# First pairs of a down projection loaded into the places of their low parts, the last column gated behind the visits, no activation sums on GpSimd

## The chip, the cores and the metric

One core of a Trainium2 chip runs the whole program. The metric is device time of one execution in microseconds; three runs of the kernel before gave 2354.93 to 2358.16, median 2356.17. Besides these there is one execution under the profiler.

## The reference, cut to what matters

One layer of a hybrid encoder over 512 + 16 prompt positions and 8 x 16 sample positions, all in float32. The change is in the last sub-layer, a convolutional gated MLP of width 5632 = 44 columns of 128:

```
up = rmsnorm(x, g_ffn) @ w_up                    # 2048 -> 2 x 5632
g, v = up[..., :D_FF], up[..., D_FF:]
gc = conv_b + sum_k gext[:, k:k + seqlen] * conv_w[k]    # causal depthwise conv, width 3
h = gelu(gc) * v
x = x + h @ w_down                               # 5632 -> 2048
```

then a final rmsnorm. Activations lie as 128 features by 640 positions (two halves of 320; the up stage carries two more columns, 322).

## The kernel before, in words

**Exact products.** Each float32 operand is split into a high part, rounded to the matmul's reduced format, and a low part, the difference; hi x hi, hi x lo and lo x hi make three matmuls. ScalarE writes the high part (`S.copy`), VectorE subtracts for the low part. For weights these are the tiles `wh` and `wl` (four buffers each) from the raw tiles `wraw` (four) and `wr` (six), each raw tile being 128 x 512 and 256 KB.

**Seven products instead of eight.** The up projection treats the input as eight pairs of feature blocks and multiplies by a Winograd scheme: seven chains (`CHAINS`) of eight pairs for the gate and value parts of a column. The seven activation combinations are kinds B11, T1, B21, B22, T3, T2, T4, kept split: pairs 0 to 5 in `XT` (pair, high or low, kind), 6 and 7 in `XH`. The weight sums P1 = A21 + A22, P3 = A11 + A21, P2 = P1 + A11, P4 = P2 + A12 are formed on VectorE in `Up.add`, four units ahead of use, and split three units ahead (a unit is half a chain, four pairs). A column is 7 x 2 x 4 x 3 = 168 matmuls. Only when P4 is formed is A11's buffer given to the next column's A11 (`free`, `load`).

**Gate.** When a column's value and gate parts are out of PSUM (`evict_up`), `gate` multiplies by the norm's scale, runs the convolution and GELU on VectorE and ScalarE, and `early` stores the column h[f] to DRAM (`h_d`) through GpSimd's queue. `gating` counts these; there are NFF = 44.

**Down projection, four parts in this order.**
- Head: columns 32 to 35 directly, 16 output rows x 4 columns x 6 matmuls = 384. `evict_head` copies a finished row from PSUM on ScalarE, `send` adds it into DRAM (`x3_d`, in the trace x_d) with an accumulating DMA on GpSimd's queue; `rows` counts.
- Sixteen visits: columns 0 to 31 as 16 pairs in the same scheme. A visit computes a pair of output rows from eight pairs; visit s uses pairs s to s + 7, so each visit brings one new pair into the place of the oldest. It has 168 matmuls of 320. The first visit runs its units in another order: first halves of five chains, then the second halves.
- REST: columns 36 to 39 directly, 384 matmuls of 320, rows evicted into `acc`.
- Tail: columns 40 to 43 in two halves of 384 and 256 positions, then the final norm.

**Where the first pairs come from.** `load_pair` takes two of the eight buffers `f26` and loads h[2p] and h[2p + 1]; `pair` forms T1, then T2, T3, T4 and splits all seven kinds into the pair's places, each behind `past(...)`, the point where column 43's matmuls have read what stood there. For pairs 0 to 9 the first sum and the split of B21 and B22 are on GpSimd (`e = G if p < KP + 2`). `some_pairs` runs two chains of three pairs; `later_pairs` does pairs 6 and 7, with GpSimd's first sums, when the head has sent eight rows and the last column is gated.

**What sets the order.** The program is written out by generators. `E.now` is the writer's estimate of the time; `E.until(E.now + 6)` holds the use of a load back by 6 us, `V.idle()` and `V.done()` hold work back while VectorE's estimated queue is long. Each engine executes its own instructions strictly in that order, as does SP, which issues nearly all loads. `room(n, gates)` waits until the next n buffers of the ring `f26` are free, and two more if gates are still to come.

Of the kernel before, what the change touches and what calls it, by code (L numbers as in the profile page):

```python
# [283 lines left out]
def body(tc, A):  # L284
# [40 lines left out]
    with tc.manual_schedule():  # L325
# [977 lines left out]
        class Up:  # L1303
# [32 lines left out]
            def add(self, u):  # L1336
                if u >= self.end:
                    return
                f, c, h = UN[u]
                p = CHAINS[c][0]  # L1340
                r = lambda n: R[f, n, h]
                if p == "P1":
                    if f == 0:
                        R[f, "P1", h] = r("A21")
                    elif f <= NFF:
                        self.put(f, "P1", h, "wraw")
                    if f <= NFF:
# [122 lines left out]

        def room(n=1, gates=False):

            while any(fl[0] + i - fpool[1] in live for i in range(n + 2 * (gates and gating[0] < NFF))):
                yield

        def let(hold):
            live.difference_update(hold)
# [39 lines left out]
        def early(f, g, v, hold):  # L1517
            while gating[0] < f:
                yield
            yield from room(2)  # L1520
            yield from gate(f, g, v, hold)
            nc.gpsimd.dma_start(out=h_d[f], in_=v[:, 0:640])  # L1522
            let(hold)
            gating[0] += 1

# [128 lines left out]
        def pair(p):  # L1654
# [22 lines left out]
            built[0] += 1  # L1677

        def some_pairs(ps):
            yield from past(-1, 2, 0)  # L1680
            yield from load_pair(ps[0])
            for p, nxt in zip(ps, ps[1:] + [None]):
                E.spawn(pair(p), 0, True)
                yield from past(-1, 6, KP - 1)
                if nxt is not None:
                    yield from load_pair(nxt)

        built = [0]
        head_at = [0]
        copied = [0]  # L1690
        rowt = [None]

        def later_pairs():
            while len(xy) < 6:
                yield
            for p in (6, 7):
                yield from load_pair(p)
# [3 lines left out]
            def two(ty, src, eng=V):  # L1701
                return split_kind([(kd(p, 0, ty), kd(p, 1, ty)) for p in (6, 7)], src, {(p, ty): p for p in (6, 7)}, eng)

            (x6, y6, hold6, _), (x7, y7, hold7, due) = xy[6], xy[7]
            xs, ys = (x6, x7), (y6, y7)
            yield from E.until(due)
            while rows[0] < 8 or gating[0] < NFF:
                yield
            place(0, B11)
            gx = fpool[0].tile([128, 18, 40], F32, tag="gx", name="gx", bufs=1).rearrange("p t b -> p (t b)")  # L1710
            t4 = gx[:, 0:320], gx[:, 320:640]
            for x in xs:
                TT(x[:, 1], x[:, 0], x[:, 1], SUB, G)
            yield from two(B11, [x[:, 0] for x in xs])
            while head_at[0] < 1:
                yield
            place(1, T1)
            yield from two(T1, [x[:, 1] for x in xs])
            for x, y, t in zip(xs, ys, t4):
                STT(x[:, 1], x[:, 1], -1.0, y[:, 1], MUL, SUB)  # L1720
                TT(t, x[:, 1], y[:, 0], ADD)
                TT(x[:, 0], x[:, 1], x[:, 0], ADD)
            while head_at[0] < 4 or rows[0] < 12:
                yield
            for i, ty, src in ((2, T4, t4), (3, T3, [x[:, 0] for x in xs]), (4, T2, [x[:, 1] for x in xs]),
                               (5, B21, [y[:, 0] for y in ys]), (6, B22, [y[:, 1] for y in ys])):
                place(i, ty)
                yield from two(ty, src)
            let(hold6 + hold7)
# [6 lines left out]

        def evict_head(n, ps):
            hold = []
            if n < 12:
                while rows[0] < n - 5:  # L1740
                    yield
                if n % 2 == 0:
                    rowt[0] = xhp.tile([128, 2, 2 * XW], F32, tag=f"xh{(0, 5, 6)[n // 2 % 3]}", name="rowt", bufs=1)
# [10 lines left out]
        def head():  # L1754

            for n in range(16):
# [20 lines left out]
        for u, (f, c, h) in enumerate(UN):  # L1777
# [54 lines left out]
            if f == NFF - 1 and h and 1 <= c <= 4:  # L1832
                load_h(HEAD[c - 1], xhp.tile([128, 2, 2 * XW], F32R, tag=f"xh{c}", name="hida", bufs=1))
                E.spawn(first_h(HEAD[c - 1], E.now + 5.5))
                if c == 1:
                    for i in range(2):
                        E.spawn(some_pairs([i, i + 2, i + 4]))
                    E.spawn(later_pairs())
# [16 lines left out]
        D = {}  # L1855

        def feed():
            while gating[0] < NFF or rows[0] < 16 + 2 * NV2:
# [18 lines left out]
            for f in last:  # L1877
                yield from split_h(f)

        E.spawn(feed())  # L1880

# [215 lines left out]
```

## Time and profile before

| | us |
|---|---|
| median of three runs | 2356.17 |
| the profiled execution | 2358.56 |
| its span, first to last instruction | 2356.8 |
| matmul engine (PE) busy | 2293.6 (97%) |
| VectorE (DVE) busy | 1869.7 (79%) |
| ScalarE (ACT) busy | 1060.2 (45%) |
| GpSimd (POOL) busy | 442.9 (19%) |
| pair loads `f<-h_d`, issue to landing, median of 46 | 4.6 |

Mean granted clock is 0.99 of full speed. PE's busy time is modelled from the starts of pipelined matmuls, so waits are read from its idle time and its clock. All matmuls and nearly all elementwise instructions share one helper line each (L164, L137); they are told apart by tiles: `pu` is a PSUM bank of the up stage, head and visits, `md` and `me` of REST and tail, `hida` and `hidb` hold split hidden columns, `f` is a buffer of the ring `f26`. Times in rows are us from the span's start. Column 42 starts at 1691.72, column 43 at 1716.38, the head at 1743.12, visit 0 at 1809.00, visit 1 at 1845.02, visit 2 at 1872.41, REST at 2225.20, the tail at 2281.75.

### The profile page before, as it was taken

Reading aid. Unit: us, or ns where it says so; the run is one execution under the profiler, and the core shown is the slowest. Engines: PE = TensorE matmul, PEld = TensorE weight load, DVE = VectorE, ACT = ScalarE, POOL = GpSimd, SP = SyncE. Lnnn points to the kernel's source line nnn. Section 1 sums busy time; section 2 is a strip of 40 time slices with the busy share of each in tenths; the row PEclk is TensorE's granted clock in tenths of the full one; section 3 lists DMA queues with packets and bytes.
Section 4 is the critical chain, followed back from the end, with each engine's and each line's share of the span. In section 5 each row is a group of like instructions: output and inputs, shape, how many; then the busy total and the mean of one; then the engine's idle time right before and its main releaser. Section 6 shows DMA issues by size and latency. Waiting matters only on the chain.

```text
span 2356.8 us, 41521 instructions
## 1 busy us (share of the span) xinstructions
PE 2293.6 (97%) x15440; PEld 2276.6 (97%) x15440; DVE 1869.7 (79%) x3084; ACT 1060.2 (45%) x1879; POOL 442.9 (19%) x640
## 2 busy tenths in 40 slices
PE   9998989999999999999999999999998899999997
PEld 9998989999999999999999999999998899999997
DVE  7589988646698888888888888888886777777646
ACT  6233443334454444444444444444454444444435
POOL 4755534200000000000000000000023211111013
PEclk9999999999999999999999999999999999999999
DMA  5323344444433333333333333333367777777643
GB/s 190 119 79 86 108 138 145 150 127 158 163 107 99 105 94 108 92 102 108 90 101 102 97 107 90 102 107 93 99 183 167 180 180 169 183 180 173 178 156 111
DMA packets 168699, 302.00 MB, mean 128 GB/s; under 512 B 22960, under 2 KB 43568, under 8 KB 168496
## 3 DMA queue, kind: packets, MB, share of 16 engines
q1 hardware_dynamic: 150784, 260.55, 35.6%
q0 software_dynamic: 17568, 38.79, 9.1%
q8 instruction: 121, 1.98, 0.3%
q14 instruction: 82, 0.67, 0.1%
q10 hardware_dynamic: 144, 0.01, 0.0%
HBM read 245.42 MB, written 53.85 MB: 127 GB/s over the span
## 4 chain that ended last, share of the span: by engine, by line
PE 78%; DVE 4%; issue 2%; ACT 1%; DMA 1%; POOL 0%; SPq 0%; DVEq 0%; POOLq 0%; ACTq 0%
PE pu L164 62%; PE mm L164 9%; PE mf L164 2%; PE me L164 2%; PE md L164 2%; DVE wl L137 1%; DVE f L137 1%; PE yps L164 1%; ACT wh L137 0%; POOL ssq L137 0%; ACT f L137 0%; DMA wr<-wup 0%; DVE acc L137 0%; PE vps L164 0%; DVE XT L137 0%
## 5 line engine op out<-in xcount | busy, mean ns | idle before, releaser
L164 PE MATMUL pu<-XT,wh 128*128 128x320 f32 (+1 forms) x5040 | 1125.1, 310 | 11.5 <-DVE f L137 8.2
L164 PEld LDWEIGHTS pu<-XT,wh 128*128 128x128 f32 x5040 | 847.4, 189 | 15.7 <-issue 10.2
L164 PE MATMUL pu<-XT,wl 128*128 128x320 f32 (+1 forms) x2520 | 781.9, 310 | 2.5 <-DVE wl L137 2.4
L137 ACT CAST wh<-wr 128x512 fp32r<-128x512 f32 x594 | 368.8, 621 | 543.6 <-PE pu L164 331.3
L137 DVE TENSOR_TENSOR wl<-wr,wh 128x512 fp32r<-128x512 f32 x594 | 411.8, 693 | 141.2 <-ACT wh L137 135.1
L164 PEld LDWEIGHTS pu<-XT,wl 128*128 128x128 f32 x2520 | 476.1, 189 | 4.4 <-DVE wl L137 4.4
L137 ACT CAST wh<-wraw 128x512 fp32r<-128x512 f32 (+1 forms) x423 | 260.2, 617 | 442.6 <-PE pu L164 159.9
L137 DVE TENSOR_TENSOR wl<-wraw,wh 128x512 fp32r<-128x512 f32 (+1 forms) x423 | 308.1, 730 | 172.2 <-ACT wh L137 168.2
L164 PE MATMUL mm<-H,wh 128*128 128x320 f32 (+2 forms) x1920 | 375.3, 317 | 12.2 <-ACT H L137 8.3
L164 PEld LDWEIGHTS mm<-H,wh 128*128 128x128 f32 x1920 | 307.3, 192 | 15.9 <-ACT H L137 8.5
L164 PE MATMUL pu<-XH,wh 128*128 128x320 f32 (+1 forms) x1232 | 276.9, 310 | 0.0
L164 PE MATMUL mm<-H,wl 128*128 128x320 f32 x960 | 223.8, 315 | 0.0
L164 PEld LDWEIGHTS pu<-XH,wh 128*128 128x128 f32 x1232 | 207.0, 189 | 0.0
L164 PE MATMUL pu<-XH,wl 128*128 128x320 f32 (+1 forms) x616 | 190.2, 309 | 0.0
L137 DVE TENSOR_TENSOR wr<-wr 128x512 f32<-128x512 f32 x236 | 162.3, 688 | 3.4
L164 PEld LDWEIGHTS mm<-H,wl 128*128 128x128 f32 x960 | 164.8, 191 | 0.0
L1499 POOL DMA_DIRECT2D cvo<-gx x44 | 31.9, 725 | 523.1 <-DVE gx L137 523.1
L137 DVE SCALAR_TENSOR_TENSOR f<-f,f 128x640 f32<-128x640 f32 (+2 forms) x161 | 123.3, 766 | 2.6 <-ACT f L137 0.8
L164 PEld LDWEIGHTS pu<-XH,wl 128*128 128x128 f32 x616 | 116.4, 189 | 0.0
L1522 POOL DMA_DIRECT2D h_d<-f x44 | 25.1, 571 | 454.4 <-DVE f L137 442.3
L137 DVE TENSOR_TENSOR wr<-wraw,wr 128x512 f32<-128x512 f32 x120 | 82.1, 684 | 0.1
L137 DVE SCALAR_TENSOR_TENSOR f<-gx,vec,f 128x640 f32<-128x640 f32 x88 | 78.8, 895 | 1.4
(299 smaller groups left out, 2890.8 us busy)
## 6 DMA issues: line engine op xcount, KB each, us to landing
wr<-wup SPq DMA_DIRECT2D x356, 256.0 KB, 2.9
wraw<-wts SPq DMA_DIRECT2D x195, 256.0 KB, 2.8
wraw<-wup SPq DMA_DIRECT2D x152, 256.0 KB, 2.8
f<-h_d SPq DMA_DIRECT2D x46, 320.0 KB, 4.6
h_d<-f POOLq DMA_DIRECT2D x44, 320.0 KB, 2.5
x_d<-f POOLq DMA_DIRECT2D x36, 320.0 KB, 4.5
wraw<-wup POOLq DMA_DIRECT2D x30, 256.0 KB, 4.3
w<-yg_d SPq DMA_DIRECT2D x16, 328.0 KB, 3.3
```

Of the source, the lines that this page charges most:

```text
L137: return f(*a, **k)
L164: return self.eng.matmul(out=out, lhsT=lhsT, rhs=rhs, start=start, stop=stop, **more)
L1499: nc.gpsimd.dma_start(out=A["cvo"][:, f], in_=gx[:, 16:18, 31:40])
L1522: nc.gpsimd.dma_start(out=h_d[f], in_=v[:, 0:640])
```

## The change

- `first_loads` / `first_load`: pairs 0 to 5 are loaded by SP straight into the pair's own places in `XT`: h[2p] into the low parts of B11 and T1 once column 43's second chain is through, h[2p + 1] into the low parts of T2 and T4 after its fifth chain has passed the pair; one pair every six units. Pairs 6 and 7 go, in eight loads of 160 KB, into `XH` places that the head's columns don't use, after column 43.
- `some_pairs` then forms the sums on VectorE into two ring buffers and splits the kinds; B11, B21 and B22 are split from where they were loaded. `later_pairs` waits for eleven sent rows, and spreads T1, T4, T3, T2 over the last head row.
- No sum or split of activations stays on GpSimd (`pair` and `later_pairs` use VectorE).
- `evict_head` takes its rows from the ring `f26` throughout, where it used three pairs of rows in `XH` places.
- P1 of the first visit is no longer summed on VectorE but by two loads on SP and two accumulating DMAs on GpSimd's queue (`Up.sum`), written at head row 13.
- Column 43: `early` stores its gate and value parts to DRAM (`u_d`); `last_gate`, started by `feed` at the start of REST, loads them, gates them and stores h[43], which is then loaded and split for the tail. The late ring has seven buffers instead of eight.

```diff
@@ Up.add
-                    elif f <= NFF:
+                    elif f < NFF:
                         self.put(f, "P1", h, "wraw")
-                    if f <= NFF:
+                    if f < NFF:
                         TT(r("P1"), r("A21"), r("A22"), ADD)
@@ room
-            while any(fl[0] + i - fpool[1] in live for i in range(n + 2 * (gates and gating[0] < NFF))):
+            while any(fl[0] + i - fpool[1] in live for i in range(n + 2 * (gates and gating[0] < NFF - 1))):
@@ early
+            if f == NFF - 1:
+                yield from V.done()
+                nc.gpsimd.dma_start(out=u_d[0][:, 0:640], in_=v[:, 0:640])
+                nc.gpsimd.dma_start(out=u_d[1][:, 0:2 * XW], in_=g.rearrange("p a c -> p (a c)"))
+                let(hold)
+                return
+        def last_gate():
+            hold = []
+            v, g = f26(hold), f26(hold)
+            SP.dma_start(out=v[:, 0:640], in_=u_d[0][:, 0:640])
+            SP.dma_start(out=g, in_=u_d[1][:, 0:2 * XW])
+            yield from E.until(E.now + 7)
+            yield from gate(NFF - 1, half2(g), v, hold)
+            nc.gpsimd.dma_start(out=h_d[NFF - 1], in_=v[:, 0:640])
+            let(hold)
+            gating[0] += 1
@@ pair
-            e = G if p < KP + 2 else V
-            TT(x[:, 1], x[:, 0], x[:, 1], SUB, e)
-            yield from e.done()
+            TT(x[:, 1], x[:, 0], x[:, 1], SUB)
+            yield from V.done()
...
-            yield from some(p, B21, y, e)
+            yield from some(p, B21, y)
@@ new, and some_pairs
+        def first_load(p):
+            f32 = lambda a, b: XT[:, p, 1, a:b, 0:320].bitcast(F32)
+            yield from past(-1, 1, p)
+            SP.dma_start(out=f32(B11, T1 + 1), in_=half2(h_d[2 * p]))
+            yield from past(-1, 4, p)
+            SP.dma_start(out=f32(T2, T4 + 1), in_=half2(h_d[2 * p + 1]))
+            xy[p] = f32(B11, T1 + 1), f32(T2, T4 + 1), None, E.now + 6
+        def first_loads():
+            for p in range(6):
+                yield from first_load(p)
+                yield 6
+            yield from past(-1, 6, 7)
...
         def some_pairs(ps):
+            for p in ps:
...
+                x, y, _, due = xy[p]
+                yield from E.until(due)
+                hold = []
+                yield from room(2, True)
+                a, b = (half2(f26(hold)[:, 0:640]) for _ in range(2))
+                TT(a[:, 0], x[:, 0], x[:, 1], SUB)
+                STT(b[:, 1], a[:, 0], -1.0, y[:, 1], MUL, SUB)
+                yield from V.idle()
+                TT(b[:, 0], b[:, 1], x[:, 0], ADD)
+                TT(a[:, 1], b[:, 1], y[:, 0], ADD)
...
@@ later_pairs
-            while rows[0] < 8 or gating[0] < NFF:
+            while rows[0] < 11 or 7 not in xy:
                 yield
...
-            while head_at[0] < 4 or rows[0] < 12:
-                yield
+            for i, ty, t in ((1, T1, t1), (2, T4, t4), (3, T3, t3), (4, T2, t2)):
+                while head_at[0] < i:
+                    yield
                 place(i, ty)
+                yield from two(ty, [t[:, 0], t[:, 1]])
@@ evict_head
-            if n < 12:
-                while rows[0] < n - 5:
-                    yield
...
-                t = rowt[0][:, n % 2]
-            else:
-                yield from room()
-                t = f26(hold)
+            yield from room(1, True)
+            t = f26(hold)
@@ head, at row 13
                     for half in range(2):
                         up.load(NFF, "A22", half)
+                    for half in range(2):
+                        up.sum(NFF, "P1", half, "A21", "A22")
@@ feed
-            fpool[1] = 8
+            fpool[1] = 7
...
-            last = range(REST[0] + 6, NFF)
-            for f in last:
-                load_h(f)
+            load_h(NFF - 2)
+            E.spawn(last_gate())
             yield from E.until(E.now + 7)
...
+            while gating[0] < NFF:
+                yield
+            load_h(NFF - 1)
+            yield from E.until(E.now + 7)
+            yield from split_h(NFF - 1)
```

## Rows read from the trace of the kernel before

**Rows 1.** Windows by stage: length; PE, PEld, DVE, ACT, POOL busy (x); PEclk, DMA, GB/s.

```profile
1691.72:1716.38 24.66, 24.66 (x170) 24.66 (x169) 21.70 (x35) 11.51 (x20) 2.07 (x4) 1.00 0.34 101
1716.38:1743.12 26.74, 24.99 (x170) 24.75 (x169) 24.17 (x38) 14.21 (x24) 3.88 (x6) 1.00 0.60 210
1743.12:1809.00 65.88, 60.26 (x386) 59.27 (x385) 43.98 (x59) 34.73 (x73) 27.37 (x28) 0.95 0.76 186
1809.00:1845.02 36.02, 28.22 (x170) 26.22 (x169) 27.95 (x50) 16.41 (x35) 7.81 (x9) 0.91 0.66 161
1845.02:1872.41 27.39, 25.23 (x171) 24.76 (x169) 23.33 (x37) 13.26 (x23) 6.41 (x6) 1.00 0.66 157
1872.41:2225.20 352.79, 349.28 (x2354) 346.26 (x2353) 271.76 (x466) 166.21 (x289) 46.97 (x54) 1.00 0.72 174
2225.20:2281.75 56.55, 56.55 (x386) 56.55 (x385) 25.48 (x36) 12.98 (x21) 0.86 (x1) 1.00 0.61 190
```

**Rows 2.** Timeline of PE: start, length, instruction, [idle before <- releaser].

```profile
1739.49 0.54 PE L164 MATMUL pu<-XT,wh 128*128 128x320 f32 x2 [1.75 <-DVE f L137]
...
1796.16 0.90 PE L164 MATMUL pu<-hida,wl 128*128 128x320 f32 x2 [4.76 <-DVE wl L137]
...
1839.95 0.87 PE L164 MATMUL pu<-XT,wh 128*128 128x320 f32 x2 [5.93 <-DVE f L137]
...
1856.91 0.41 PE L164 MATMUL pu<-XT,wh 128*128 128x320 f32 x1 [1.44 <-DVE XT L137]
```

**Rows 3.** Windows of 10 us around the head's long wait, same columns.

```profile
1790.00:1800.00 10.00, 5.24 (x24) 4.99 (x23) 8.11 (x6) 2.75 (x5) 5.54 (x5) 0.77 0.70 166
1800.00:1810.00 10.00, 9.45 (x57) 9.19 (x56) 1.81 (x1) 2.58 (x7) 3.38 (x5) 0.89 0.50 125
```

**Rows 4.** Timelines of DVE and POOL before that wait ended.

```profile
1789.24 1.62 DVE L137 TENSOR_TENSOR f<-f,f 128x320 f32<-128x320 f32 x1
1790.79 5.31 DVE L137 TENSOR_TENSOR wl<-wraw,wh 128x512 fp32r<-128x512 f32 x1
...
1791.07 4.47 POOL L137 TENSOR_TENSOR XT<-f,XT 128x640 fp32r<-128x640 f32 x3
```

**Rows 5.** Groups by form in the head: count | busy us, mean ns | idle before.

```profile
L137 DVE TENSOR_TENSOR XT<-f,XT 128x640 fp32r<-128x640 f32 x11 | 9.7, 886 | 5.5 <-ACT XT L137 5.5
...
L137 DVE TENSOR_TENSOR f<-f 128x320 f32<-128x320 f32 x5 | 2.5, 492 | 0.2
```

**Rows 6.** Timelines of DVE, SP's queue and ACT in visit 0.

```profile
1830.81 0.69 DVE L137 TENSOR_TENSOR wr<-wr 128x512 f32<-128x512 f32 x1
...
1831.87 0.33 SPq L1310 DMA_DIRECT2D wr<-wup  x1
...
1837.54 0.62 ACT L137 CAST wh<-wr 128x512 fp32r<-128x512 f32 x1 [3.30 <-DMA wr<-wup]
```

**Rows 7.** Timeline of ACT in column 43.

```profile
1736.24 0.73 ACT L137 CAST hida<-hida 128x640 fp32r<-128x640 f32 x1 [2.63 <-DMA hida<-h_d]
...
1737.39 0.42 ACT L137 COPY u<-pu 128x320 f32<-128x320 f32 x1
```

**Rows 8.** DMA issues from 1715 to 1870: count, KB each, median us to landing.

```profile
f<-h_d SPq DMA_DIRECT2D x22, 320.0 KB, 6.1
...
wraw<-wup POOLq DMA_DIRECT2D x4, 256.0 KB, 4.3
```

**Rows 9.** Timelines of DVE (the last column's gate), ACT and PE (REST and tail).

```profile
1747.76 0.89 DVE L137 TENSOR_TENSOR gx<-f,rstd 128x640 f32<-128x640 f32 x2
...
1759.48 1.68 DVE L137 SCALAR_TENSOR_TENSOR f<-f,f 128x640 f32<-128x640 f32 x2 [0.82 <-ACT f L137]
...
2240.01 0.73 ACT L137 CAST hida<-hida 128x640 fp32r<-128x640 f32 x1 [7.17 <-DMA hida<-h_d]
...
2288.05 0.69 PE L164 MATMUL me<-hidb 128*128 128x384 f32 x3
```

**Rows 10.** Waits of POOL from 1720 to 1870: us in total, times, longest.

```profile
POOL f L137 <- DMA f<-h_d: 34.0, 6, 10.4
```

More of the change, by code (lines that the diff above doesn't have):

```diff
@@ L1674, in pair @@
             yield from V.idle()
-            yield from some(p, B21, y, e)
+            yield from some(p, B21, y)
             let(hold)
-            built[0] += 1
-        def some_pairs(ps):
[L1680 to L1686, printed above, removed]
@@ L1688, in body @@
-        built = [0]
+        def first_load(p):
[10 more added lines that the diff above has]
+            yield from past(-1, 6, 7)
+            raw = lambda ty, i, h: XH[ty][:, i, h, 0:320].bitcast(F32)
+            for i in range(2):
+                x, y = h_d[2 * (6 + i)], h_d[2 * (6 + i) + 1]
+                x0, x1, y0, y1 = raw(B11, i, 1), raw(B11, i, 0), raw(B21, i, 1), raw(B22, i, 1)
+                for o, t, c in ((x0, x, 0), (x1, x, 320), (y0, y, 0), (y1, y, 320)):
+                    SP.dma_start(out=o, in_=t[:, c:c + 320])
+                xy[6 + i] = x0, x1, y0, y1, E.now + 6
@@ new lines, in some_pairs @@
+        def some_pairs(ps):
+            for p in ps:
+                while p not in xy:
+                    yield
[9 more added lines that the diff above has]
+                TT(a[:, 1], b[:, 1], y[:, 0], ADD)
+                yield from V.idle()
+                yield from some(p, B11, x[:, 0:1])
+                yield from V.idle()
+                yield from some(p, T1, a[:, 0:1])
+                yield from past(-1, 6, p)
+                yield from V.idle()
+                yield from some(p, B21, y)
+                yield from V.idle()
+                yield from some(p, T3, b)
+                yield from V.idle()
+                yield from some(p, T4, a[:, 1:2])
+                let(hold)
@@ L1689, in body @@
         head_at = [0]
         copied = [0]
-        rowt = [None]
         def later_pairs():
-            while len(xy) < 6:
-                yield
-            for p in (6, 7):
-                yield from load_pair(p)
             def place(i, ty):
                 XH[ty] = xhp.tile([128, 2, 2, XW], F32R, tag=f"xh{i}", name=f"XH{ty}b", bufs=1)
[L1701 to L1706, printed above, removed]
-            while rows[0] < 8 or gating[0] < NFF:
-                yield
[L1709 to L1715, printed above, removed]
-                yield
[L1717 to L1722, printed above, removed]
-            while head_at[0] < 4 or rows[0] < 12:
-                yield
-            for i, ty, src in ((2, T4, t4), (3, T3, [x[:, 0] for x in xs]), (4, T2, [x[:, 1] for x in xs]),
-                               (5, B21, [y[:, 0] for y in ys]), (6, B22, [y[:, 1] for y in ys])):
@@ new lines, in two @@
+            def two(ty, src):
+                return split_kind([(kd(p, 0, ty), kd(p, 1, ty)) for p in (6, 7)], src, {(p, ty): p for p in (6, 7)})
+            while rows[0] < 11 or 7 not in xy:
+                yield
+            yield from room(4)
+            hold = []
+            t1, t2, t3, t4 = (half2(f26(hold)[:, 0:640]) for _ in range(4))
+            for i in range(2):
+                x0, x1, y0, y1, due = xy[6 + i]
+                yield from E.until(due)
+                TT(t1[:, i], x0, x1, SUB)
+                STT(t2[:, i], t1[:, i], -1.0, y1, MUL, SUB)
+                yield from V.idle()
+                TT(t3[:, i], t2[:, i], x0, ADD)
+                TT(t4[:, i], t2[:, i], y0, ADD)
+                yield from V.idle()
@@ L1727, in later_pairs @@
+            lo = lambda ty: [XH[ty][:, i, 1, 0:320].bitcast(F32) for i in range(2)]
+            yield from V.done()
+            yield from two(B11, lo(B11))
+            for i, ty, t in ((1, T1, t1), (2, T4, t4), (3, T3, t3), (4, T2, t2)):
+                while head_at[0] < i:
+                    yield
                 place(i, ty)
-                yield from two(ty, src)
-            let(hold6 + hold7)
+                yield from two(ty, [t[:, 0], t[:, 1]])
+            let(hold)
+            for ty in (B21, B22):
+                yield from two(ty, lo(ty))
@@ L1738, in evict_head @@
             hold = []
-            if n < 12:
-                while rows[0] < n - 5:
-                    yield
-                if n % 2 == 0:
-                    rowt[0] = xhp.tile([128, 2, 2 * XW], F32, tag=f"xh{(0, 5, 6)[n // 2 % 3]}", name="rowt", bufs=1)
-                t = rowt[0][:, n % 2]
-            else:
-                yield from room()
-                t = f26(hold)
+            yield from room(1, True)
+            t = f26(hold)
             for (o, w), p in zip(HP, ps):
@@ L1835, in body @@
                 if c == 1:
+                    E.spawn(first_loads())
                     for i in range(2):
@@ L1857, in feed @@
         def feed():
-            while gating[0] < NFF or rows[0] < 16 + 2 * NV2:
+            while gating[0] < NFF - 1 or rows[0] < 16 + 2 * NV2:
                 yield
@@ L1872, in feed @@
             E.spawn(rest_acc())
-            last = range(REST[0] + 6, NFF)
-            for f in last:
-                load_h(f)
+            load_h(NFF - 2)
+            E.spawn(last_gate())
             yield from E.until(E.now + 7)
-            for f in last:
-                yield from split_h(f)
+            yield from split_h(NFF - 2)
+            while gating[0] < NFF:
+                yield
+            load_h(NFF - 1)
+            yield from E.until(E.now + 7)
+            yield from split_h(NFF - 1)
         E.spawn(feed())
```

## The prediction, made before the changed kernel ran

> **What bounds the kernel now.** I read the page first: the matmul engine is busy 97% of the span, so a change can only win where it stands still or runs at the lower clock. The windows cut at the program's stages come next [rows 1]. Column 42 is an undisturbed column of the up stage: 24.66 us. The last column, 43, takes 26.74. The direct part ("head") of the down stage takes 65.88, but the later direct part of columns 36 to 39 does the same 384 matmuls of 320 columns without a wait in 56.55. The first visit takes 36.02, the second 27.39; visits 2 to 15 take 352.79 / 14 = 25.20 each. The excess is 2.08 + 9.33 + 10.82 + 2.19 = 24.42 us, all in the 156 us that the change edits. That is the most it can win there; the visits behind keep their shape.
>
> Then the matmul engine's own waits [rows 2]: 1.75 us in column 43, 4.76 in the head, 5.93 in visit 0, 1.44 in visit 1, each put down to VectorE. After a wait the clock falls: the 10 us around the long head wait were granted 0.77 of full speed and the next ten 0.89 [rows 3], 81 matmuls where two full slices hold about 140. The missing 59, at 24.66/170 = 0.145 us, are 8.6 us: nearly all of the head's excess is this one wait and its slow echo.
>
> **The head: sums leave GpSimd.** The late instruction is one weight subtraction on VectorE that lasts 5.31 us, beside three GpSimd subtractions of 4.47 us together that began 0.28 us later; the sum just before it took 1.62 us against 0.49 on average for its shape [rows 4, 5]. The change puts every such subtraction on VectorE, so this stretch, the 4.76 wait and the slow clock behind it go. What comes instead: six two-part subtractions at 0.82 to 0.89 us (5.3) and, with the eight first sums, 8 x 0.49 (3.9) [rows 5].
>
> Is there room on VectorE? It is busy 43.98 us in the head [rows 1]. From that go the 8.5 us or so by which instructions ran longer beside GpSimd (4.6 and 1.1 in [rows 4], 1.2 for each of two in the gate and for a weight split, 0.3 at the end), and the last column's gate, 5.9 us (seven instructions of 0.8 to 0.9). To the rest, 29.6, come 4.9 + 2.5 of GpSimd's work inside the stage, six sums of pairs 6 and 7 (2.9), four of their seven splits (3.6), and 2 to 3 us of pairs 0 and 1 done in column 43 so far: 46 us of 56.55. It fits with 10 us over. I leave 2.5 us of the 9.33: 1.0 for first sums in front of a load not yet landed, 1.0 for the first visit's P1 (below), 0.5 at the ends. Bounds: 0.5 (all hidden) and 9.3 (as now).
>
> **P1 of visit 0** was two VectorE sums (0.7 each, one stretched to 1.3); it becomes two loads on SP and two accumulating DMAs on GpSimd's queue, issued at row 13 of 16. They need the weight buffers that the last two head chunks hold, so SP stands until VectorE has split these, and GpSimd's queue, with the row stores behind it, stands until each load has landed. An accumulating load of this size lands 4.3 us after issue here [rows 8]. With chunk 14 split about 12 us before the head's end, a load of some 4 and an accumulation of 4.3 to 5, P1 arrives 2 to 3 us before its split must begin: bounds 0 and 4 us of wait, I take 1.0. The Trainium skill ("DMA: Bandwidth & Descriptors", Anatomy of one DMA) puts a GpSimd DMA at 2.0 us plus its bytes over 436 GB/s, which for 256 KB is an estimated 2.6 us. The rows show 4.3, and by the page's figure the 1.0 would be 0.
>
> **Visit 0.** The chain of its long wait [rows 6]: VectorE forms the last weight sum (A12 + P2) at 1830.81; only that frees the buffer into which SP loads the next visit's A11 at 1831.87; the cast of it on ScalarE waits 3.30 us for the landing and starts at 1837.54, and the copy of a finished bank stands behind this cast, VectorE's combination behind that, and the matmuls behind that. In program order the weight sum belongs beside the unit that starts 14 us into the visit (about 1824.5 with the early waits); it came some 6 us late, behind VectorE's own queue (27.95 us busy in this visit [rows 1], nearly all before the wait). From there go P1's sums (2.0), six sums of pairs 6 and 7 (2.9), three or four of their splits at 0.89 (3.1), and stretched instructions (2.5): 10 us. Then the load is issued in time, and what is left is the short order of this visit: the copy and three VectorE operations, 1.8 us, against one unit of 1.76 us between. I leave 3.0 of 10.82. Bounds: 0.3, and 10.8 if the load is late for another reason.
>
> **Column 43.** The finished bank's copy came at 1737.39, behind a cast that waited 2.63 us for a hidden column's load [rows 7]. That load queued behind four pair loads (320 KB each); in the changed order one pair half stands ahead of it, the second halves come after chain 4, and then one pair every six units. A few hundred KB less is about 1 us. I leave 1.0 of 2.08; bounds 0, and 4 if the crowded queue gets slower.
>
> **Visit 1** waits for pair 8's T4 part [rows 2]; its load is issued when pairs 6 and 7 are finished, which is now earlier: 1.2 of 2.19 stay, bounds 0 and 3.
>
> **The last column's gate moves to the REST stage.** It issues two stores on GpSimd, two more loads, its arithmetic, a store, and the load of column 43 again on SP. VectorE is busy 25.48 of 56.55 us there [rows 1], so 5.9 us fit. In time: the old load of that column was cast from 2240.01 on after a 7.17 us wait, and first needed at 2288.05 [rows 9]. The gate ran from 1747.76 to 1761.16, 13.4 us [rows 9]; store and reload at 7.2 each, SP behind a chunk load 3.5, split 1.6: 2241.5 + 32.9 = 2274, 14 us to spare. I put 0.7 for VectorE or ScalarE standing before a load (bounds 0 and 3). The tail's ring of seven buffers instead of eight costs nothing: its squares are taken up one after another by GpSimd's sums, and these pace it.
>
> **The sum.** Left: 1.0 + 2.5 + 3.0 + 1.2 + 0.7 = 8.4 against 24.42, a gain of 16.0. The profiled execution was 2358.56 (span 2356.8): 2342.6. The median of the runs is 2.39 below it: 2340. All bounds at their best leave 0.8 us (2332.6); all at their worst leave 30, a loss of 6 (2362).
>
> **Rivals.**
> A. *VectorE inherits GpSimd's waits.* GpSimd stood 34.0 us in six waits for pair loads, the longest 10.4 [rows 10]; it could afford to. The program starts a pair 6 us after its load is issued, and the median landing in this stretch is 6.1 [rows 8]. At 2 us late for each of eight pairs, 16 us, VectorE's 10 us of room are gone; 6 stop the matmuls, and a slow clock adds 1. 2347. For it: over the whole run the page has 4.6 for such loads, so this stretch is crowded. Against: four pairs' loads move forward, out of the head. The Trainium skill (same page, Issuing engines are not separate DMA queues) says that DMAs of all issuers share the same 16 engines. By it the P1 accumulation and the early loads delay each other, which is this case.
> B. *Visit 0 keeps its wait*, because the A11 load is slow itself (5.7 us from issue to cast) and not issued late: 7.8 us of the gain are lost, 2348. Against it: the weight sum itself was 6 us late.
> A and B together: 2354, no change.
> C. *Slower.* The loads land as the slowest did: 10.4 us, 4.4 late, eight times, 35 us in front of weight splits on VectorE. Less 10 of room, 25 us stop the matmuls, with 1 to 2 us of slow clock: 16 - 26.5 = -10, 2366. It decides from a mean lateness of (10 + 16 + 4.7)/8 = 3.8 us. Against it: one wait of six was that long.
> D. *The change does not do what it says*: head rows now take their buffers from the same eight as the pairs, so copies queue and the PSUM ring of four rows fills. It takes a copy 10.6 us late (three rows) to stop a matmul; its price then is the head's gain, 7, and it counts with A.
>
> **How the numbers follow.** A measurement here tells about 0.2%, 4.7 us, from no change. Forecast 0.60 (2333 to 2346, likeliest 2340); A or D 0.09 (2347); B 0.09 (2348); A with B 0.12 (2354); C 0.10 (2366). Faster 0.60 + 0.09 + 0.09 = 0.78, same 0.12, slower 0.10. The range reaches from the best bounds, with 1 us for changed waits in the later visits, to A with B: 2332 to 2354.
>
> **What would show it.** Right: no GpSimd subtractions between column 43 and visit 1, no VectorE weight split over 1 us in the head, granted clock 1.00 through it, a head under 60 us, visit 0 under 29, column 43's second load cast before 2275. A is shown by VectorE waits named for pair loads; B by a cast in visit 0 that still waits for a weight load; P1's step fails if the cast of P1 waits for GpSimd's DMA for over 2 us. A head above 66 us, or matmuls that wait for column 43 in the tail, would make the prediction wrong.

## The result, and the profile after

The changed kernel takes 2335.91 us (median of 4 runs, 2335.04 to 2338.56) against 2357.16 for the kernel before on the same chip: 0.9919 of its time, 95% interval 0.9907 to 0.9932. A second set of runs (below) gave 0.9924 [0.9911, 0.9936]. The forecast was 2340 us, with 2332 to 2354 as the range. The profiled execution took 2335.62, with a span of 2333.8; 3.5 us of its 23 us against the profiled one before lie ahead of column 43, where the programs are the same: column 43 starts at 1712.86 instead of 1716.38 [rows 1], after a clock that was granted 0.97 instead of 0.93 and 0.90 in two 50 us windows of the up stage. The 13 profiled executions of this study that share the program up to there and ran after the forecast start column 43 anywhere from 1712.06 to 1716.84. So I compare stages, not spans.

Windows by stage of the changed kernel, columns and stages as in [rows 1] without its column 42 (column 43, head, visits 0, 1, 2 to 15, REST):

```profile
1712.86:1738.30 25.44, 25.01 (x171) 24.77 (x170) 22.72 (x38) 12.17 (x21) 1.96 (x4) 1.00 0.63 219
1738.30:1795.23 56.93, 56.79 (x387) 56.53 (x386) 41.41 (x81) 37.01 (x83) 14.35 (x18) 1.00 0.93 231
1795.23:1824.37 29.14, 26.40 (x170) 26.16 (x169) 22.43 (x42) 14.74 (x30) 4.46 (x6) 0.94 0.90 217
1824.37:1849.43 25.06, 24.95 (x171) 24.72 (x169) 20.88 (x37) 12.72 (x22) 3.48 (x4) 1.00 0.69 171
1849.43:2202.03 352.60, 349.32 (x2355) 346.30 (x2353) 271.72 (x466) 166.44 (x290) 46.98 (x54) 1.00 0.72 174
2202.03:2258.51 56.48, 56.48 (x386) 56.48 (x385) 30.99 (x44) 14.72 (x25) 2.92 (x4) 1.00 0.67 209
```

The head lost its excess, visit 0 most of its own, and GpSimd's busy time in the head fell from 27.37 to 14.35 us [rows 1]. VectorE's busy time there fell by 2.6 us: the gate's work and the stretching left it, the sums came. From column 43 to visit 1 two waits of the matmul engine over 0.25 us remain. The kernel before had eight there, of which [rows 2] shows the four longest (timeline of PE):

```profile
1734.66 0.54 PE L164 MATMUL pu<-XT,wh 128*128 128x320 f32 x2 [0.43 <-DVE f L137]
...
1819.33 0.87 PE L164 MATMUL pu<-XT,wh 128*128 128x320 f32 x2 [2.74 <-DVE f L137]
```

The chain behind the second, which answers to [rows 6], is first a cast and a copy on ScalarE (timeline of ACT):

```profile
1815.13 0.62 ACT L137 CAST wh<-wr 128x512 fp32r<-128x512 f32 x1 [0.90 <-DMA wr<-wup]
1815.65 0.42 ACT L137 COPY u<-pu 128x320 f32<-128x320 f32 x1
```

and then VectorE's queue (timeline of DVE):

```profile
1815.78 0.69 DVE L137 TENSOR_TENSOR wl<-wr,wh 128x512 fp32r<-128x512 f32 x1 [1.45 <-ACT wh L137]
1816.39 0.82 DVE L137 TENSOR_TENSOR XT<-f,XT 128x640 fp32r<-128x640 f32 x1
1817.24 0.49 DVE L137 SCALAR_TENSOR_TENSOR f<-f,f 128x320 f32<-128x320 f32 x1
1817.77 0.49 DVE L137 TENSOR_TENSOR f<-f 128x320 f32<-128x320 f32 x1
1818.18 0.48 DVE L137 TENSOR_TENSOR u<-pu,u 128x320 f32<-128x320 f32 x1
```

The weight load waits 0.90 us where it had waited 3.30, the bank is copied by 1816.07, and VectorE then does a split and three operations of pair 8 before it combines the bank at 1818.18.

The loads into the low parts' places are slow in this execution, 8.4 us from issue to landing in the median, with the DMA engines 1.00 busy from 1722 to 1744, where most are issued, and 0.93 in the head (DMA issues from 1711 to 1866, columns as in [rows 8]):

```profile
XT<-h_d SPq DMA_DIRECT2D x12, 320.0 KB, 8.4
wraw<-wup POOLq DMA_DIRECT2D x8, 256.0 KB, 4.3
...
XH<-h_d SPq DMA_DIRECT2D x8, 160.0 KB, 8.3
```

In the other eight executions with direct loads, shown below, the first median is 6.2 to 7.8 us. Though the loads were slow, VectorE waited for none of them between column 43 and visit 1 in this execution. It did wait 3.9 us for a ring buffer that a row store still held, the mechanism of rival D, and no matmul waited for that:

```profile
DVE f L137 <- DMA x_d<-f: 3.9, 1, 3.9
```

### The profile page after: what moved, and what is told of

It is laid out like the page before. It is cut to its first block, busy times and chain, and to the rows that moved or that the text cites. A ratio compares the mean times of both kernels' runs of the same rounds, so it can differ in the third digit from the quotient of the medians.

```text
span 2333.8 us, 41535 instructions
## 1 busy us (share of the span) xinstructions
PE 2283.7 (98%) x15440; PEld 2269.5 (97%) x15440; DVE 1861.8 (80%) x3106; ACT 1060.0 (45%) x1885; POOL 422.5 (18%) x626
## 4 chain that ended last, share of the span: by engine, by line
PE 79%; DVE 3%; issue 1%; DMA 1%; ACT 1%; POOL 1%; SPq 0%; DVEq 0%; POOLq 0%; ACTq 0%
PE pu L164 63%; PE mm L164 9%; PE mf L164 2%; PE me L164 2%; PE md L164 2%; DVE f L137 1%; DVE wl L137 1%; PE yps L164 1%; POOL ssq L137 0%; ACT wh L137 0%; DVE acc L137 0%; PE vps L164 0%; DMA x_d<-f 0%; ACT f L137 0%; DMA hida<-h_d 0%
## 5 line engine op out<-in xcount | busy, mean ns | idle before, releaser
L137 DVE TENSOR_TENSOR wl<-wraw,wh 128x512 fp32r<-128x512 f32 (+1 forms) x423 | 301.7, 714 | 167.6 <-ACT wh L137 163.8
L164 PE MATMUL pu<-XH,wh 128*128 128x320 f32 (+1 forms) x1424 | 320.1, 310 | 2.3 <-DVE f L137 2.3
L164 PEld LDWEIGHTS pu<-XH,wh 128*128 128x128 f32 x1424 | 239.1, 189 | 3.0 <-ACT wh L137 3.0
L164 PE MATMUL pu<-XH,wl 128*128 128x320 f32 (+1 forms) x712 | 219.9, 309 | 0.0
L164 PEld LDWEIGHTS pu<-XH,wl 128*128 128x128 f32 x712 | 134.5, 189 | 0.0
L1548 POOL DMA_DIRECT2D x_d<-f x48 | 42.0, 912 | 236.0 <-DVE f L137 203.2
```

Of the source, the lines that this page charges most:

```text
L137: return f(*a, **k)
L164: return self.eng.matmul(out=out, lhsT=lhsT, rhs=rhs, start=start, stop=stop, **more)
L1548: nc.gpsimd.dma_start(out=x3_d[n], in_=half2(t[:, 0:640]), accum_op=ADD)
```

## The experiments

Each ratio is against the kernel before, run beside it on the same chip, where its medians were 2355.0 to 2357.2; so ratios compare better than medians. Stage lengths are from each run's one profiled execution, cut at the same matmuls; undisturbed are 24.7 for column 43 or visit 0, 25.1 for visit 1, 56.5 for the head.

```
run                       median   ratio [95%]               col 43  head   visit 0  visit 1
before                    2357.16                            26.74   65.88   36.02   27.39
changed                   2335.91  0.9919 [0.9907, 0.9932]   25.44   56.93   29.14   25.06
e6_changed_again          2338.06  0.9924 [0.9911, 0.9936]   28.83   56.53   29.40   25.07
e1_gpsimd_sums            2339.21  0.9931 [0.9918, 0.9943]   25.54   56.52   31.27   26.07
e2_v_sums_only            2351.83  0.9983 [0.9974, 0.9992]   28.96   58.57   31.87   27.89
e4_gate_moved_only        2344.84  0.9958 [0.9945, 0.9970]   26.74   58.10   32.74   26.14
e5_all_but_direct_loads   2343.37  0.9949 [0.9935, 0.9962]   28.89   56.66   31.73   25.68
e5_p1_on_vector           2336.86  0.9922 [0.9910, 0.9935]   26.63   56.52   28.79   25.06
e8_due_two                2341.37  0.9944 [0.9931, 0.9958]   31.60   56.53   29.78   25.08
e3_before_unit_order      2351.86  0.9984 [0.9975, 0.9993]   26.31   65.79   31.47   27.79
e7_unit_order             2332.07  0.9905 [0.9892, 0.9919]   26.11   56.52   24.74   25.08
e10_unit_order_again      2332.23  0.9901 [0.9888, 0.9915]   26.36   56.53   24.73   25.08
e9_late_column_casts      2337.33  0.9920 [0.9907, 0.9932]   24.77   61.58   24.74   25.07
e11_column_ahead          2333.15  0.9903 [0.9889, 0.9917]   24.78   58.13   24.73   25.08
```

**GpSimd's sums put back.**

```diff
-            TT(x[:, 1], x[:, 0], x[:, 1], SUB)
+            e = G if p < KP + 2 else V
+            TT(x[:, 1], x[:, 0], x[:, 1], SUB, e)
...
-            yield from some(p, B21, y)
+            yield from some(p, B21, y, e)
...
-                TT(a[:, 0], x[:, 0], x[:, 1], SUB)
+                TT(a[:, 0], x[:, 0], x[:, 1], SUB, G)
...
```

> The changed kernel with the first sums of the pairs (x0 - x1) and the pairs' B21 splits put back on GpSimd; loads, gate and P1 stay as changed. Theory (two-input operations of GpSimd beside VectorE's stretch both, and that was the head's loss): at least one VectorE weight split or sum in the head lasts over 2 us beside them, the matmuls wait 2 to 5 us and the clock falls behind it: 5 to 10 us slower than the changed kernel, 2341 to 2346. Rival (the loads, the moved gate and the room on VectorE carry the gain, whoever sums): 0 to 2 us slower, 2336 to 2338.

The time lies 1 to 3 us above the changed kernel's two medians, less than the theory's 5 to 10 and at the upper end of the rival's 0 to 2; the intervals overlap. The head kept its 56.52. GpSimd did 16.9 us of subtractions in it (groups of 11.0, 3.8 and 2.1), and VectorE was stretched as before (groups by form in the head):

```profile
L137 DVE TENSOR_TENSOR XT<-f,XT 128x320 fp32r<-128x320 f32 x12 | 13.8, 1156 | 1.7 <-ACT XT L137 1.6
L137 DVE TENSOR_TENSOR wl<-wraw,wh 128x512 fp32r<-128x512 f32 x16 | 12.3, 771 | 2.3 <-ACT wh L137 2.3
```

Twelve splits at 1.156 instead of 0.488 us are 8.0 us of stretching, and no matmul waited. So GpSimd beside VectorE is not by itself the head's loss. What was stretched is mostly splits of activations. The longest weight split there (timeline of DVE) is far from the 5.31 us of [rows 4], so the theory's condition, a weight split or sum of over 2 us, did not come about (the longest sum took 1.58):

```profile
1749.64 1.54 DVE L137 TENSOR_TENSOR wl<-wraw,wh 128x512 fp32r<-128x512 f32 x1 [1.58 <-ACT wh L137]
```

The 1.9 to 2.1 us in visit 0 and 1.0 in visit 1 are what the edit costs here.

**Two parts of the change alone, and all but one.** The first has only the sums on VectorE, the second only the moved gate (with its ring of seven), the third both and P1's accumulation, without the direct loads.

```diff
-            e = G if p < KP + 2 else V
+            e = V
...
-                TT(x[:, 1], x[:, 0], x[:, 1], SUB, G)
+                TT(x[:, 1], x[:, 0], x[:, 1], SUB)
```

> The kernel before with only this changed: the pairs' first sums and B21 splits on VectorE instead of GpSimd (two lines). Gate, loads, buffers and P1 as before. Theory: the 5.31 us weight split, its 4.76 us wait and the slow clock behind it go, 7 to 9 us in the head, and 0 to 2 us in visit 0, whose wait mostly stays since VectorE still carries everything else: 2346 to 2350. Rival (without the moved gate VectorE has no room for the sums, so its own queue stops the matmuls): under 3 us of gain, 2354 or more.

```diff
+            if f == NFF - 1:
+                yield from V.done()
+                nc.gpsimd.dma_start(out=u_d[0][:, 0:640], in_=v[:, 0:640])
...
+            E.spawn(last_gate())
```

> The kernel before with only the last column's gate moved behind the visits; GpSimd still sums, P1 is still VectorE's, loads as before. Theory 1 (GpSimd's subtractions beside VectorE's are the head's loss, each by itself): they still stretch a weight split by several us, the head stays above 62 us, 2350 to 2355. Theory 2, from the run with GpSimd's sums put back into the changed kernel, whose head took 56.52 us beside 17 us of GpSimd subtractions: the stretching costs only where VectorE has no room for it; without the gate's 5.9 us it has, and the head takes under 60 us, 2344 to 2349.

> The kernel before with GpSimd's sums on VectorE, the last column's gate moved behind the visits, and the first visit's P1 accumulated by DMA; the loads of the pairs, their buffers and the order of pairs 6 and 7 as before. Theory: the head is as in the changed kernel within 2 us; the direct loads are worth what pairs 6 and 7, summed in visit 0, cost there (3 to 5 us), and about 1 us in column 43: 2340 to 2342. Rival (the direct loads are worth nothing once GpSimd is quiet): 2336 to 2338.

In microseconds of 2356 the ratios are gains of 4.0, 9.9 and 12.0; the changed kernel has 18 to 19. The sums alone, at 2351.83, come out between their theory (2346 to 2350) and rival (2354 or more); all but the direct loads, at 2343.37, 1.4 us above their theory. The gate alone is the largest part, with GpSimd still summing: theory 2 of that run held in its time, 2344.84, and its head, 58.10. But its reason, room, did not: VectorE is as busy in that head as before (44.03 against 43.98 us), and the head is 7.8 us shorter. What differs is how the subtractions fall. Before, the last three of one form stood in a row and held one weight split for 5.31 us [rows 4]. With the gate gone the last three of that form come apart (timeline of POOL):

```profile
1779.30 1.76 POOL L137 TENSOR_TENSOR XT<-f,XT 128x640 fp32r<-128x640 f32 x1
1782.04 1.75 POOL L137 TENSOR_TENSOR XT<-f,XT 128x640 fp32r<-128x640 f32 x1
1785.57 1.77 POOL L137 TENSOR_TENSOR XT<-f,XT 128x640 fp32r<-128x640 f32 x1
```

No weight split lasts over 2.5 us (timeline of DVE):

```profile
1761.46 2.49 DVE L137 TENSOR_TENSOR wl<-wraw,wh 128x512 fp32r<-128x512 f32 x1 [0.65 <-ACT wh L137]
...
1785.84 2.06 DVE L137 TENSOR_TENSOR wl<-wraw,wh 128x512 fp32r<-128x512 f32 x1 [1.09 <-ACT wh L137]
```

With the sums alone on VectorE the profiled head is 58.57: in these executions either part is enough for the head, so their gains don't add. One thing stays open there: that profiled execution, at 2347.90, was the fastest of 11 (up to 2355.25), and its stages show more than twice the gain of the median; what the others lost was not seen. The direct loads are worth the rest, 6 to 7 us by the ratios; in the stages 2.3 to 2.6 of it are in visit 0 and 0.6 in visit 1, where the theory had 3 to 5 and the rival nothing. Column 43 is no witness: it took 25.44 and 28.83 us in two executions of the changed kernel itself. So 3 to 4 us of the direct loads' worth are not located.

**P1 on VectorE again.**

```diff
-                    elif f < NFF:
+                    elif f <= NFF:
                         self.put(f, "P1", h, "wraw")
-                    if f < NFF:
+                    if f <= NFF:
                         TT(r("P1"), r("A21"), r("A22"), ADD)
...
-                    for half in range(2):
-                        up.sum(NFF, "P1", half, "A21", "A22")
```

> The changed kernel with the first visit's P1 summed on VectorE again (two sums of 0.7 us) instead of accumulated by DMA. Theory: these two sums come back into the stretch before VectorE's weight sum for the next A11, where 1.4 us count fully in visit 0's wait: 1 to 2 us slower than the changed kernel, 2337 to 2338. Rival: VectorE has room there, 0, or the two fewer 256 KB accumulations in a stretch with the DMA engines at 0.90 let the A11 load land earlier and it gains 1 us.

Level with the changed kernel beside it (2338.06): the rival. If the accumulation costs or gains anything, it is less than these runs tell; visit 0 takes 28.79 us here against 29.14 and 29.40.

**The changed kernel again.**

> The changed kernel once more, on the same chip as the runs beside it. It should take 2334 to 2338, and its profile should show the stage lengths of the first (column 43 25.4, head 56.9, visit 0 29.1, visit 1 25.1 us) within 1 us each, while the start of column 43 may differ by 3 us, as it did between the executions so far (1712.86 to 1716.84) with the same program up to there.

The time, 2338.06, lies at the upper end. Head and visits agree within 0.4 us. Column 43 missed by 3.4: its wait was 2.33 us instead of 0.43. A finished bank's copy stands behind a cast whose load lands late, as in [rows 7] (timelines of ACT and PE):

```profile
1732.43 0.73 ACT L137 CAST hida<-hida 128x640 fp32r<-128x640 f32 x1 [3.76 <-DMA hida<-h_d]
...
1733.58 0.42 ACT L137 COPY u<-pu 128x320 f32<-128x320 f32 x1
...
1735.76 0.54 PE L164 MATMUL pu<-XT,wh 128*128 128x320 f32 x2 [2.33 <-DVE f L137]
```

In the first execution that cast waited 1.86 us. The clock fell behind the wait (windows of 4 us, columns as in [rows 1]):

```profile
1732.00:1736.00 4.00, 1.67 (x12) 1.43 (x11) 2.71 (x6) 2.71 (x5) 0.00 (x0) 1.00 1.06 389
1736.00:1740.00 4.00, 4.00 (x18) 4.00 (x18) 3.93 (x9) 1.21 (x3) 0.56 (x1) 0.57 1.07 382
1740.00:1744.00 4.00, 4.00 (x30) 4.00 (x29) 3.96 (x9) 0.93 (x3) 0.54 (x1) 1.00 1.04 372
```

After a window with 1.67 us of matmuls the grant is 0.57 of full speed, near the lower of the two levels (1.2 of 2.4 GHz): 18 matmuls where 30 fit.

**Sums in front of loads that have not landed.**

```diff
-            xy[p] = f32(B11, T1 + 1), f32(T2, T4 + 1), None, E.now + 6
+            xy[p] = f32(B11, T1 + 1), f32(T2, T4 + 1), None, E.now + 2
...
-                xy[6 + i] = x0, x1, y0, y1, E.now + 6
+                xy[6 + i] = x0, x1, y0, y1, E.now + 2
```

> The changed kernel with the pairs' sums put 2 us behind their loads' issue instead of 6. The loads land 8.4 us after issue (median), so VectorE stands about 4 us longer at up to eight of them, some 32 us in all. The prediction's rivals A and C reckon such waits against VectorE's room: by its figures the matmuls stop for what is over it. With the 15 us of room that the changed kernel's head shows (41.4 busy of 56.9): 32 - 15 = 17 us, about 2354. Rival (the planner puts other work between, and a wait costs only where a weight split stands right behind it): 0 to 5 us, 2336 to 2342.

The rival's 2336 to 2342, and not where either placed it: the head keeps 56.53, and column 43 takes 31.60. One sum, put ahead of the combination of a finished bank, waited for its load (DVE's timeline), and the matmuls stood 3.97 us for that combination:

```profile
1734.55 0.49 DVE L137 SCALAR_TENSOR_TENSOR f<-f,XT 128x320 f32<-128x320 f32 x1 [4.30 <-DMA XT<-h_d]
...
1736.30 0.48 DVE L137 TENSOR_TENSOR u<-pu,u 128x320 f32<-128x320 f32 x1
```

VectorE's waits for these loads were this one alone, not 32 us. Two things differ from what the expectation reckoned with: the loads landed after 6.3 us (median) in this run and not 8.4, and the sums that were moved stand among other work that was late already, which is read from the program and not shown by a run.

**Another order of units in visit 0,** in the changed kernel (twice) and in the kernel before:

```diff
-        UN[U0:U0 + 14] = [(NFF, c, h) for c, h in ((0, 0), (1, 0), (2, 0), (3, 0), (5, 0), (0, 1), (1, 1), (2, 1), (3, 1),
-                                                   (4, 0), (4, 1), (5, 1), (6, 0), (6, 1))]
+        UN[U0:U0 + 14] = [(NFF, c, h) for c, h in ((0, 0), (1, 0), (2, 0), (3, 0), (0, 1), (1, 1), (2, 1), (3, 1),
+                                                   (4, 0), (4, 1), (5, 0), (5, 1), (6, 0), (6, 1))]
```

> The changed kernel with another order of the first visit's 14 units: chain 5's first unit goes behind both units of chain 4 instead of ahead of the second half, so two units lie between the end of chain 4 and the unit that waited 2.74 us at 1819.33. Theory (what is left of visit 0's excess is the short order: copy and three VectorE operations against one unit of 1.76 us): that wait falls by 1.5 to 2.7 us and the slow clock behind it goes too, 2 to 4 us faster than the changed kernel, 2332 to 2334. Rival (the wait is VectorE's backlog or the late A11 cast at 1815.13, whatever the order): the wait only moves to another unit, 0 to 1 us, 2335 to 2337.

> The kernel before with nothing changed but the order of the first visit's units (chain 5's first unit behind both units of chain 4, as in the run with the changed kernel that took visit 0 to 24.74 us). The prediction's theory for the old 5.93 us wait (a late weight sum behind VectorE's backlog, so that the A11 load was issued some 6 us late): the new order gives at most its own 1.8 us, visit 0 stays at 33 to 36 us, the kernel gains 0 to 3 us, 2352 to 2355. Rival (the short order is the cause and the late load only shows in it): visit 0 falls below 30 us, 6 us or more gained, 2349 or less.

> The changed kernel with the new unit order in visit 0 once more, beside the run with the later casts on the same chip: 2330 to 2334, visit 0 under 25.5 us, and column 43 between 25.4 and 28.9 us.

In the changed kernel the theory held, with 2332.07 and 2332.23, and visit 0 has no wait left (its window):

```profile
1799.47:1824.21 24.74, 24.74 (x170) 24.74 (x169) 21.95 (x42) 14.66 (x30) 4.57 (x6) 1.00 1.01 245
```

Two units now cover what one of 1.76 us had to. On the kernel before the order gains 3.8 us, 4.55 in visit 0, between theory and rival: the 5.93 us wait goes, and the next thing late is a split of pairs 6 and 7, at 31.47 us for the visit (PE's timeline):

```profile
1823.76 0.42 PE L164 MATMUL pu<-XH6b,wh 128*128 128x320 f32 x1 [2.44 <-DVE XH6b L137]
```

So of visit 0's old excess of 11.3 us over 24.74 the order held 4.4 to 4.7 in either kernel and the parts of the change the other 6.7 to 6.9, and with both gone it is gone.

**Column 43.** On top of the new order, first the casts later, then also the pairs' loads behind the head's fourth column:

```diff
-                E.spawn(first_h(HEAD[c - 1], E.now + 5.5))
+                E.spawn(first_h(HEAD[c - 1], E.now + (9 if c < 4 else 5.5)))
```

```diff
                 yield from first_load(p)
+                if p == 0:
+                    yield from past(-1, 5, 0)
```

> The changed kernel with the new unit order in visit 0 and, besides, the casts of the first three of the head's columns put 9 us behind their loads' issue instead of 5.5. Theory: column 43's wait (0.43 to 2.33 us in three runs, with the clock at 0.57 for 4 us behind the longest) is the copy of a finished bank that stands on ScalarE behind a cast whose load lands late, at DMA engines that are busy throughout; with the casts behind the copy it goes, column 43 takes 25 us instead of 25.4 to 28.8 and the kernel gains 1 to 3 us on the new unit order alone, about 2330 to 2331. Rival: the wait moves to a weight cast or to the head's first row, 0 us, 2332 to 2333.

> As the run with the new unit order and the later column casts, and besides the loads of pairs 1 to 5 begin only after the head's fourth column has been sent for, which moves two loads of 320 KB from in front of that column's load to behind it. In the run without this the fourth column's cast waited 6.22 us and stopped the head for 2.49. Theory (that wait is the place in SP's queue at DMA engines that are busy throughout): two loads of 320 KB at the 380 GB/s moved there are 1.7 us, so the column lands 1.5 to 2.5 us earlier, the head's wait falls under 1 us and column 43 stays at 24.8: 2329 to 2332, level with or 1 to 2 us under the new unit order alone. Rival (the pairs, now later, become the head's or visit 0's wait): no gain on the new unit order alone or a loss of 1 to 3 us, 2333 to 2336.

Column 43 is undisturbed (24.77), so its wait was the copy behind a cast. But the first run is 5 us slower than the order alone, where the theory had 1 to 3 faster and the rival no change: the wait moved, as the rival said, though to another place, and grew. The fourth column's cast waits for its load (timeline of ACT):

```profile
1743.06 0.73 ACT L137 CAST hida<-hida 128x640 fp32r<-128x640 f32 x1 [6.22 <-DMA hida<-h_d]
```

and the head stops for it, with the clock at 0.71 and 0.87 in the two 4 us windows from 1744 on (timeline of PE):

```profile
1744.83 0.71 PE L164 MATMUL pu<-hida,wh 128*128 128x320 f32 x3 [2.49 <-DVE hida L137]
```

In the second run that load stands ahead of two others in SP's queue, and the same cast waits less (timeline of ACT):

```profile
1739.03 0.73 ACT L137 CAST hida<-hida 128x640 fp32r<-128x640 f32 x1 [2.22 <-DMA hida<-h_d]
```

which leaves the head 0.58 us (timeline of PE):

```profile
1743.42 0.71 PE L164 MATMUL pu<-hida,wh 128*128 128x320 f32 x3 [0.58 <-DVE hida L137]
```

Each step took away the wait it was for, but the sum, 2333.15, is level with the new order alone, at the edge of its rival's range. The best version found is that order by itself: 2332.1, about 4 us under the changed kernel by the medians (two ratios each; their intervals overlap by a little).

## Why the prediction was right

**The size.** The forecast gain was 16.0 us in the edited stretch: the changed kernel's two profiled executions show 19.5 and 16.2 from column 43 to visit 1 against 156.03 us before, and the ratios 18 to 19. The terms left over, against the two executions: column 43 1.0 (0.8 and 4.2), head 2.5 (0.4 and 0.0), visit 0 3.0 (3.9 and 4.2 over the 25.20 used there), visit 1 1.2 (-0.1 and -0.1), REST 0.7 (-0.1 and -0.1). They sum to 4.9 and 8.2 against 8.4. That the sum is nearer than the single terms is luck: the head, visit 1 and REST were put too high, visit 0 too low, and column 43 too low in the second execution. Of the signs named beforehand one failed: visit 0 was to be under 29 us and took 29.14 and 29.40. Rivals A and B together come to 2355 by their own prices, not 2354; nothing hangs on that.

**The head.** Right that the stretch, its wait and the slow clock behind it go, and that VectorE has room (41.4 us busy; 46 reckoned). What fell is the weight on room. It explained why taking over the sums would be harmless, and that held. But the gate's move was costed in the head only as 5.9 us of room, while by itself it gains 9.9 us in time; its profiled stages show 12.3, of them 7.8 in the head. What the rows show of the loss is one bunch of GpSimd subtractions beside a weight split that the matmuls wait for. In the run with the gate moved, weight splits of 2.06 and 2.49 us stopped no matmul, and one of 1.36 us is ahead of a wait of 0.99. The runs do not show what tied the bunch to the gate, only that it comes apart without it. A head can carry 8 us of stretching in pieces, at least on splits of activations.

**P1.** Its 1.0 us was for accumulations that arrive late. GpSimd's queue did stand, 6.19 and 2.48 us for the two loads (POOL's timeline), with three row stores behind it, and the matmuls never noticed:

```profile
1789.31 0.87 POOL L1334 DMA_DIRECT2D wraw<-wup  x1 [6.19 <-DMA wraw<-wup]
1792.67 0.87 POOL L1334 DMA_DIRECT2D wraw<-wup  x1 [2.48 <-DMA wraw<-wup]
1793.21 3.01 POOL L1548 DMA_DIRECT2D x_d<-f  x3
```

The accumulations landed 4.3 us after issue (median of eight), as the row said. The Trainium skill's figure ("DMA: Bandwidth & Descriptors", Anatomy of one DMA), an estimated 2.6, is not what these runs show; their P1 had slack for either.

**Visit 0.** The short order was named and mis-sized: the copy and three operations, 1.8 us against a unit of 1.76, forgot 1.8 us of pair 8's work ahead of the combination and 0.9 for the weight load. That wait measured 2.74, with 1.7 of slow clock behind it (over the undisturbed 24.74), and the run with another order took all of it away. The forecast's chain came half true. The A11 load is issued in time now, 14.8 us into the visit instead of 22.9. But the order decides what a late load costs: in the kernel before with the new order it is issued as late as ever, 22.9 us into the visit, and no matmul waits for it (SP's queue, that run first, then the changed kernel):

```profile
1829.90 0.33 SPq L1310 DMA_DIRECT2D wr<-wup  x1
...
1810.06 4.62 SPq L1310 DMA_DIRECT2D wr<-wup  x4
```

VectorE's backlog was real too, but by another way than the A11 load: what is left in that run is a wait of 1.35 us for a weight split at the visit's start, the 2.44 us for a split of pairs 6 and 7, and slow clock.

**Column 43.** Its one value hid a spread: the wait hangs on when two loads land at fully busy DMA engines. The second execution took 4.2, a little over the bound of 4 for a crowded queue.

**REST.** VectorE took the gate in (25.48 to 30.99 us busy). The last column's second load was cast at 2240.71, 38.7 us into REST, and no matmul waited; the limit set, 2275 in the times of the trace before, is 49.8 us into it:

```profile
2240.71 0.73 ACT L137 CAST hidb<-hidb 128x640 fp32r<-128x640 f32 x1 [6.36 <-DMA hidb<-h_d]
```

**The rivals.** A reckoned with VectorE waits for pair loads: none came, although in the first execution loads landed 2.4 us later than the program allowed for (0.5 in the second). So the allowance was not the margin. C's price stays untested: with the sums 4 us earlier VectorE waited 4.3 us and not 32 to 35. What the one wait shows is that VectorE's room in a stage does not take it up where a bank's combination stands right behind: the matmuls stood 3.97 us, in column 43. B's wait for the weight load shrank from 3.30 to 0.90, so it did not hold. The Trainium skill (same page, Issuing engines are not separate DMA queues) has all queues share the DMA engines. The medians of a 320 KB load, 8.4 and 6.5 us in the two executions of the changed kernel against 6.1 before [rows 8], lie too far apart to show what that sharing costs here.

## What to carry to other kernels

Price a second engine's interference by the longest bunch that falls beside an operation with little lead; the sum of stretched time did not tell the loss here. Where a finished bank must be copied and combined before a later unit can start, count everything that the program has put between on both engines; here one unit was too little and two were enough. And where DMA engines are full, a wait taken away at one load can turn up at another, as at the head's fourth column here, so look there before counting the gain.

## What the runs showed that was not expected

- One GpSimd subtraction of 1.7 to 1.8 us (128 x 640) beside a VectorE weight split of 0.69 makes that 2.06 us; one behind a sum of 1.16 us makes it 2.49, and three in a row make it 5.31 [rows 4]. In the head with the sums put back, 16.9 us of GpSimd subtractions cost VectorE 8.0 us in one group of splits alone.
- What a wait of the matmuls in column 43 cost beyond itself, over the undisturbed 24.77 us: 0.2 us at 0.43 to 1.75 us (eight executions, granted clock 1.00 over the column), 1.5 to 1.7 us at 2.33 to 2.66 (three, 0.94), 2.9 us at 3.97 (0.89), where the clock stood at 0.56 and 0.58 of full speed over 8 us.
- The same program, up to column 43, differs by 4.8 us between executions; head and visits of the changed kernel repeat within 0.4 us, column 43 does not (25.44 and 28.83).
